# Low parts last, a late unit behind the squares, transposes one piece later: reordering the passes of a split-float32 encoder trunk

## The chip, the cores and the metric

The kernel runs on one core of a Trainium2 chip, in one launch. The metric is the device time of the execution in microseconds (us). The matrix engine is called TensorE (PE in the profile; its loads of the stationary operand are PEld), the others are VectorE (DVE), ScalarE (ACT), GpSimd (POOL) and SyncE (SP), whose queue starts the transfers.

## The reference, cut to what matters

Two layers work on 256 tokens of 1024 numbers. Each layer has parallel branches, a feed-forward part and an embedding part, with a norm before and behind each.

```python
def hybrid_layer(h, p_i, ...):
    u = rms_norm(h, g_mix_pre)
    (gq, gk, gv, gg, ra_f, ra_b, aq, ak, av, gate_a, gate_b) = jnp.split(u @ w_in, offsets, axis=-1)
    # branch A: gated linear attention, both directions, times silu(gg), @ w_o_gla
    # branch B: grouped-query attention with rotary positions, @ w_o_attn
    mixed = jax.nn.sigmoid(gate_a) * branch_a + jax.nn.sigmoid(gate_b) * branch_b
    h = h + rms_norm(mixed @ w_out, g_mix_post)

    gate, up = jnp.split(rms_norm(h, g_ffn_pre) @ w_ffn_in, 2, axis=-1)
    h = h + rms_norm((jax.nn.silu(gate) * up) @ w_ffn_out, g_ffn_post)

    e = p_i @ w_ple_proj
    h = h + rms_norm(jax.nn.sigmoid(h @ w_ple_gate) * e, g_ple_post)
    return h
```

Everything is float32.

## The kernel before, in words

**Products in three passes.** Every float32 operand of a large product is split into a high part (a rounded copy, `fp32r`) and a low part (the rest). A product x*y is the sum of three passes on TensorE: xh*yh, xh*yl and xl*yh. `mm3` issues these three for one block of 128 of the inner dimension, and the next block follows. `split` makes the parts: ScalarE copies to the high part (`nc.scalar.copy`, line 118, a CAST in the profile), and VectorE subtracts it from the source to make the low part (`vsub`, line 114). A low part is thus always made after its high part.

**Units of weights.** The weights come as units: 2048 (in the rank/query stage 2112) columns of 128 rows, four blocks of 128 by 512, 1 MB. A plan lists the units in the order of use. `Stream` moves them: a transfer fills a `raw` buffer (two of them), `put` takes a pair of places `wh` and `wl` (four pairs), and `fill` splits the unit in two pieces of half its columns. `take` hands out the next unit, and `done` says that its last product has been issued: it counts the unit out (`held`), starts transfers that have room, and calls `fill`, which splits the next unit as long as fewer than `depth` (4, at times 3) are held. A raw buffer is free for the next transfer when VectorE has made the low part of its second piece.

**Products.** The tokens are two halves (`hf` 0 and 1) of 128. `amode` multiplies one half's activations with 512 or 256 columns of one unit; the activations are the stationary operand. `wmode` takes the weights as the stationary operand. `times` is used for the seven products of a block scheme, `rq_step` for the first stage of a layer (ranks and queries), where a step is one unit of one half, in three blocks of 288, 384 and 384 columns, two blocks of the inner dimension each, 18 passes in all. `by_half` is used for the output projection (`wout`) and for the embedding gate (`gate`, tiles named `ple` in the profile): it takes four units, does the first token half with all of them, then the second half, and there the second 512 columns are done as two pieces of 256. Each unit is counted out in the second half, as its last piece ends. `then` follows each half: `after_out` or `after_gate`, a norm behind the product, the addition to `h` and the norm before the next product.

**Norm chain.** The norm (`row_rstd`, `pre_norm`, `post_norm_add`) takes the squares of two halves of a row on ScalarE (line 460), an addition and a power on GpSimd (lines 472 and 476), and a scaling on VectorE (line 480 ahead of the next product, 520 for the addition to `h`). The result is transposed on TensorE (`transpose_in`, line 422) and split into the activations of the next product. `last_square` keeps the last square that was issued.

**Order.** The order of each engine's queue is set when the kernel is built: instructions of earlier program order go first when they are ready by a modelled time, `tc.high_priority` moves the norm chains ahead, and `tc.issue_after(x)` holds an instruction behind x in its engine's queue. Deferred work (transposes above all) lives in tasks; a product calls `tick` after each half unit, or after each 256-column piece or each block of `rq_step`, and a task that was told to wait n ticks issues its work at the n-th. The constants `WAIT...` at the top are these numbers. In the layer change, `pre_norm(gnext, hf, nxt, (WAIT, WAIT_NEXT)[hf])` gives the first half's transposes 6 ticks and the second half's 9. Of the second half's gate pieces each 512-column one gives two ticks and each 256-column one gives one, eight in all. The steps of layer 1's first stage are, as half and unit, `00 01 02 10 03 11 12 13`.

## Time and profile before

| | |
|---|---|
| median of 3 runs | 929.62 us (928.83 to 929.95) |
| the profiled execution | 930.95 us |
| its span, first to last instruction | 929.2 us |
| mean granted TensorE clock | 0.996 |
| TensorE busy | 915.3 us, 4669 passes and transposes |
| loads of the stationary operand | 777.1 us, 4669 |
| VectorE busy | 787.3 us |
| ScalarE busy | 580.5 us |
| GpSimd busy | 88.1 us |
| read from memory | 167.41 MB, 181 GB/s over the span |

Busy times come from the one profiled execution. Matmuls overlap in it and their ends are modelled, so starts are the better measure: the time from one start to the next. A row of the timeline gives the start, the length, the engine, the line and operation, output and inputs by the program's names (`wl_0ple` is a low part that was made in layer 0 in the part `ple`), the shapes, the count of instructions merged into the row, and in brackets the idle time before it with what ended it.

### The profile page before, as it was taken

The page shows a single profiled execution, that of the slowest core. Times are in us where ns is not written, and L with a number is a line of the kernel's source. Part 1 is how long each engine was busy: PE and PEld are TensorE (multiplying, and loading weights), DVE is VectorE, ACT ScalarE, POOL GpSimd, SP SyncE. Part 2 cuts the span into 40 slices and gives each one's busy share as a digit, 9 for nine tenths or more (in the row PEclk, how much of TensorE's full clock was granted, in tenths as well). Part 3 has the DMA queues.
Part 4 walks back from the last instruction along what each step waited for, and adds up shares of the span by engine and source line. Part 5 has one row for each costly group of instructions (what it writes and reads, how often), then busy time and mean ns, then how long its engine had stood idle before and what let it go on. Part 6 is the DMA issues. An engine that isn't in the chain of part 4 may idle for free.

```text
span 929.2 us, 12392 instructions
## 1 busy us (share of the span) xinstructions
PE 915.3 (99%) x4669; PEld 777.1 (84%) x4669; DVE 787.3 (85%) x1002; ACT 580.5 (62%) x955; POOL 88.1 (9%) x147
## 2 busy tenths in 40 slices
PE   8999999999999999999999999999999999999996
PEld 6898888888878888888889988888888788888886
DVE  6898989987679898998779789899786899989974
ACT  4669676664466565666656686755545666655663
POOL 3400212310000000001022002200001000000000
PEclk9999999999999999999999999999999999999999
DMA  7463445556385564627545525354663847473551
GB/s 264 138 240 122 154 164 187 178 201 230 107 271 190 182 245 174 228 102 268 182 138 182 185 88 172 113 214 139 246 226 114 287 139 265 159 256 129 182 182 45
DMA packets 88247, 169.25 MB, mean 182 GB/s; under 512 B 3374, under 2 KB 26550, under 8 KB 88188
## 3 DMA queue, kind: packets, MB, share of 16 engines
q1 hardware_dynamic: 88028, 168.32, 52.4%
q8 instruction: 36, 0.59, 0.3%
q10 hardware_dynamic: 160, 0.15, 0.1%
q14 instruction: 23, 0.19, 0.1%
HBM read 167.41 MB, written 1.05 MB: 181 GB/s over the span
## 4 chain that ended last, share of the span: by engine, by line
PE 89%; DVE 3%; DMA 2%; ACT 2%; POOL 2%; issue 2%; SPq 0%; POOLq 0%; DVEq 0%; ACTq 0%
PE acc_0ffnin L102 11%; PE acc_1ffnin L102 11%; PE acc_0ffnin L566 6%; PE acc_1ffnin L566 6%; PE acc_0gate L102 5%; PE acc_1gate L102 5%; PE acc_1gqk L102 2%; PE acc_0gqk L102 2%; PE acc_1ple L102 2%; PE acc_0gg L102 2%; PE acc_1gg L102 2%; PE acc_1v L102 2%; PE acc_0v L102 2%; PE acc_1merge L102 2%; PE acc_0merge L102 2%; PE acc_1gate L566 2%
## 5 line engine op out<-in xcount | busy, mean ns | idle before, releaser
L102 PE MATMUL acc_1ffnin<-wh_1ffnin,big_1ffnin 128*128 128x512 f32 x176 | 56.8, 392 | 0.0
L102 PE MATMUL acc_0ffnin<-wh_0ffnin,big_0ffnin 128*128 128x512 f32 x176 | 56.8, 392 | 0.0
L118 ACT CAST wh_0ffnin<-raw_0ffnin 128x1024 fp32r<-128x1024 f32 x38 | 38.2, 1050 | 23.9 <-DVE wl_0ffnin L114 6.9
L114 DVE TENSOR_TENSOR wl_0ffnin<-raw_0ffnin,wh_0ffnin 128x1024 fp32r<-128x1024 f32 x38 | 44.9, 1220 | 8.3 <-ACT wh_0ffnin L118 8.3
L118 ACT CAST wh_1ffnin<-raw_1ffnin 128x1024 fp32r<-128x1024 f32 x38 | 38.1, 1049 | 21.6 <-DMA raw_1ffnin<-in_w_ffn_out_dram 7.0
L114 DVE TENSOR_TENSOR wl_1ffnin<-raw_1ffnin,wh_1ffnin 128x1024 fp32r<-128x1024 f32 x38 | 44.9, 1221 | 7.3 <-ACT wh_1ffnin L118 7.2
L102 PEld LDWEIGHTS acc_1ffnin<-wh_1ffnin,big_1ffnin 128*128 128x128 f32 x176 | 33.0, 188 | 6.7
L102 PEld LDWEIGHTS acc_0ffnin<-wh_0ffnin,big_0ffnin 128*128 128x128 f32 x176 | 33.0, 188 | 6.7
L114 DVE TENSOR_TENSOR wl_1ffnin<-lent_1ffnin,wh_1ffnin 128x1024 fp32r<-128x1024 f32 x30 | 35.9, 1219 | 1.9 <-ACT wh_1ffnin L118 1.9
L114 DVE TENSOR_TENSOR wl_0ffnin<-lent_0ffnin,wh_0ffnin 128x1024 fp32r<-128x1024 f32 x30 | 35.9, 1219 | 1.7 <-ACT wh_0ffnin L118 1.7
L102 PE MATMUL acc_0ffnin<-wl_0ffnin,big_0ffnin 128*128 128x512 f32 x88 | 34.3, 389 | 0.0
L102 PE MATMUL acc_1ffnin<-wl_1ffnin,big_1ffnin 128*128 128x512 f32 x88 | 34.3, 389 | 0.0
L118 ACT CAST wh_1ffnin<-lent_1ffnin 128x1024 fp32r<-128x1024 f32 x30 | 30.2, 1053 | 6.5 <-PE acc_1ffnin L102 3.0
L118 ACT CAST wh_0ffnin<-lent_0ffnin 128x1024 fp32r<-128x1024 f32 x30 | 30.1, 1053 | 6.0 <-PE acc_0ffnin L102 3.0
L566 PE MATMUL acc_0ffnin<-wh_0ffnin,mid_0ffnin 128*128 128x512 f32 x96 | 31.1, 391 | 0.0
L566 PE MATMUL acc_1ffnin<-wh_1ffnin,mid_1ffnin 128*128 128x512 f32 x96 | 31.1, 391 | 0.0
L102 PE MATMUL acc_1ffnin<-wh_1ffnin,big_1wout 128*128 128x512 f32 x96 | 31.0, 393 | 0.0
L102 PE MATMUL acc_0ffnin<-wh_0ffnin,big_0wout 128*128 128x512 f32 x96 | 31.0, 393 | 0.0
L114 DVE TENSOR_TENSOR wl_1gate<-raw_1gate,wh_1gate 128x1024 fp32r<-128x1024 f32 x20 | 23.6, 1220 | 6.2 <-ACT wh_1gate L118 6.1
L114 DVE TENSOR_TENSOR wl_0gate<-raw_0gate,wh_0gate 128x1024 fp32r<-128x1024 f32 x20 | 23.8, 1234 | 5.2 <-ACT wh_0gate L118 5.2
L118 ACT CAST wh_1gate<-raw_1gate 128x1024 fp32r<-128x1024 f32 x20 | 20.2, 1051 | 12.7 <-DMA raw_1gate<-in_w_o_attn_dram 6.4
L118 ACT CAST wh_0gate<-raw_0gate 128x1024 fp32r<-128x1024 f32 x20 | 20.1, 1052 | 12.2 <-DMA raw_0gate<-in_w_o_attn_dram 5.9
(697 smaller groups left out, 2999.1 us busy)
## 6 DMA issues: line engine op xcount, KB each, us to landing
raw_0ffnin<-in_w_ffn_out_dram SPq DMA_DIRECT2D x11, 1024.0 KB, 5.1
raw_1ffnin<-in_w_ffn_out_dram SPq DMA_DIRECT2D x11, 1024.0 KB, 5.8
lent_0ffnin<-in_w_ffn_in_dram SPq DMA_DIRECT2D x6, 1024.0 KB, 7.5
lent_1ffnin<-in_w_ffn_in_dram SPq DMA_DIRECT2D x6, 1024.0 KB, 7.5
raw_0v<-in_w_in_dram SPq DMA_DIRECT2D x4, 1024.0 KB, 4.9
raw_0gate<-in_w_o_gla_dram SPq DMA_DIRECT2D x4, 1024.0 KB, 5.0
raw_0gate<-in_w_o_attn_dram SPq DMA_DIRECT2D x4, 1024.0 KB, 5.5
raw_0wout<-in_w_ffn_in_dram SPq DMA_DIRECT2D x8, 512.0 KB, 4.6
```

Source lines behind the costliest of these rows:

```text
L102: return nc.tensor.matmul(o, lhsT, rhs, start=start, stop=stop)
L114: nc.vector.tensor_tensor(out=out, in0=in0, in1=in1, op=ALU.subtract)
L118: nc.scalar.copy(hi, src)
L566: nc.tensor.matmul(o, x, y, start=first and k + n == 0, stop=k == 3 and n == 2, skip_group_check=not first)
```

## The change

Three things are changed.

1. `passes` takes the place of `mm3` in `amode`, `wmode`, `times` and `rq_step`. It issues the same passes in another order: for each block of the inner dimension the two passes that do not use the part named last, and behind all blocks the passes with that part. With `fresh` that part is the low part of the first operand (the activations, or in `wmode` the weights), otherwise the low part of the second (the weights, where the activations are stationary). `fresh` is set for the first 512 columns in `by_half`, for the first block of the feed-forward part, for the first unit in `rq_step`, and in `wmode`. `rq_first`, `out_step` and the attention keep their order. The ticks stay where they were: after half of the passes and at the end.
2. `by_half` is called with `early`. The last unit that it counts out is no longer refilled at once: `fill` runs after `then` of the second half, and the ScalarE copies of the unit it splits are held behind the last square. A class `Early`, counts of large tiles and a flag `go` are added, by which units could be split into large tiles ahead of time; no item of the plan is such a unit.
3. In the layer change the first half's transposes wait 7 ticks instead of 6.

```diff
-WAIT, WAIT_FIRST, WAIT_NEXT, WAIT_H, WAIT_FFN, WAIT_BLOCK = 6, 4, 9, 5, 4, 6
+WAIT, WAIT_FIRST, WAIT_H, WAIT_FFN, WAIT_BLOCK = 6, 4, 5, 4, 6
+
+WAIT_NEXT = 7, 9
...
+    def passes(o, parts, start, stop, fresh=False, between=None, **kw):
+        ps = [((xh, yh), (xh, yl), (xl, yh)) if fresh else ((xh, yh), (xl, yh), (xh, yl)) for (xh, xl), (yh, yl) in parts]
+        seq = [p for t in ps for p in t[:2]] + [t[2] for t in ps]
+        for n, (x, y) in enumerate(seq):
+            nc.tensor.matmul(o, x, y, start=start and n == 0, stop=stop and n == len(seq) - 1, **kw)
+            if between is not None and 2 * (n + 1) == len(seq):
+                between()
...
-        def fill(self):
-            while self.open and self.held < self.depth and self.jobs:
+        def fill(self, behind=None):
+            while self.open and self.jobs and (self.go if self.jobs[0] in self.early else self.held < self.depth):
                 pieces = self.jobs.pop(0)()
-                for piece in pieces or ():
-                    split(*piece)
+                for hi, lo, src in pieces or ():
+                    with tc.issue_after(behind) if behind is not None else nullcontext():
+                        nc.scalar.copy(hi, src)
+                    vsub(lo, src, hi.bitcast(F32))
                 if pieces:
                     self.load()
...
-        def done(self, n=1):
-            self.held -= n
+        def done(self, n=1, late=False):
+            self.go = False
+            for _ in range(n):
+                self.held -= self.taken.pop(0)
             self.start()
-            self.fill()
+            if not late:
+                self.fill()
...
-    def amode(o, sp, hf, k0, w, first, last, c0=0):
+    def amode(o, sp, hf, k0, w, first, last, c0=0, fresh=False):
...
-        for k in range(4):
-            mm3(o, sp.tok(k0 + k, hf), (wh[:, k, :], wl[:, k, :]), first and k == 0, last and k == 3)
-            if k % 2 and (k == 3 or o.shape[-1] == 512):
-                tick()
+        parts = [(sp.tok(k0 + k, hf), (wh[:, k, :], wl[:, k, :])) for k in range(4)]
+        passes(o, parts, first, last, fresh, tick if o.shape[-1] == 512 else None)
+        tick()
...
-    def by_half(sp, then):
+    def by_half(sp, then, early=False):
...
-                    amode(t, sp, hf, kh * 4, us[kh, min(j, 1)], kh == 0, kh == 1, 256 * (j == 2))
+                    amode(t, sp, hf, kh * 4, us[kh, min(j, 1)], kh == 0, kh == 1, 256 * (j == 2), j == 0)
+                    if hf == 0 and kh == 1 and early:
+                        ws.go = True
+                        ws.fill()
                     if hf == 1 and j != 1:
-                        ws.done()
+                        ws.done(late=early and (kh, j) == (1, 2))
             then(hf, o)
+        if early:
+
+            ws.fill(last_square[0].ins)
...
-            for k in range(2):
-                s = slice(k * 1056 + c0, k * 1056 + c1)
-                mm3(
-                    o[:, : c1 - c0], uT.tok(2 * u + k, hf), [t[:, s] for t in us[u]],
-                    u == 0 and k == 0, u == 3 and k == 1,
-                )
+            s = [slice(k * 1056 + c0, k * 1056 + c1) for k in range(2)]
+            parts = [(uT.tok(2 * u + k, hf), [t[:, s[k]] for t in us[u]]) for k in range(2)]
+            passes(o[:, : c1 - c0], parts, u == 0, u == 3, u == 0)
             tick()
...
-        by_half(mixT, after_out)
+        by_half(mixT, after_out, True)
...
-                pre_norm(gnext, hf, nxt, (WAIT, WAIT_NEXT)[hf])
+                pre_norm(gnext, hf, nxt, WAIT_NEXT[hf])
...
-        by_half(hT, after_gate)
+        by_half(hT, after_gate, True)
```

More of the change, by code (lines that the diff above doesn't have):

```diff
@@ L283, in put @@
         def put(self, x, parts=2):
[L285 to L288 removed]
             cuts = [slice(j * x.n // parts, (j + 1) * x.n // parts) for j in range(parts)]
+            if x.bigs == 4:
+                ts = [big(F32R)[:, : x.n // parts] for _ in range(4)]
+                self.ready.append((ts[0:2], ts[2:4], 0))
+                return [(ts[j], ts[2 + j], x.raw[:, c]) for j, c in enumerate(cuts)]
+            if x.bigs:
+                wh, wl = big(F32R), big(F32R)
+            else:
+                wh = wp.tile([P, UNIT], F32R, tag="wh", name=nm("wh"))
+                wl = wp.tile([P, UNIT], F32R, tag="wl", name=nm("wl"))
+                self.held += 1
+            self.ready.append((wh, wl, not x.bigs))
             return [(wh[:, c], wl[:, c], x.raw[:, c]) for c in cuts]
@@ L548, in wmode @@
             s = slice(f * P, (f + 1) * P)
-            for k in range(4):
-                mm3(
-                    o, (wh[:, k, s], wl[:, k, s]), sp.all(k0 + k),
-                    first and k == 0 and f % 2 == 0, last and k == 3 and f % 2 == 1,
-                )
+            parts = [((wh[:, k, s], wl[:, k, s]), sp.all(k0 + k)) for k in range(4)]
+            passes(o, parts, first and f % 2 == 0, last and f % 2 == 1, True)
             tick()
@@ L561, in times @@
         wh, wl = (t[:, :2048].rearrange("p (k c) -> p k c", c=512) for t in ws.take())
-        for k in range(4):
-            (ah, al), h, lo = act(k), wh[:, k, :], wl[:, k, :]
-            for n, (x, y) in enumerate(((ah, h), (ah, lo), (al, h))):
-                nc.tensor.matmul(
-                    o, x, y, start=first and k + n == 0, stop=k == 3 and n == 2, skip_group_check=not first
-                )
-            if k % 2:
-                tick()
+        parts = [(act(k), (wh[:, k, :], wl[:, k, :])) for k in range(4)]
+        passes(o, parts, first, True, between=tick, skip_group_check=not first)
+        tick()
         if then:
```

28 lines of the change are left out of this document (15 added, 13 removed).

## The prediction

> **What bounds the kernel now.** First the page's part on busy time, then the waits of TensorE, then two stretches by windows, then the timelines of the places that the waits name.
>
> ```profile
> PE 915.3 (99%) x4669; PEld 777.1 (84%) x4669; DVE 787.3 (85%) x1002; ACT 580.5 (62%) x955; POOL 88.1 (9%) x147
> ...
> 297.04 2.72 PE acc_0ffnin L102 x12
> ...
> 68.17 5.76 PE acc_0gqk L102 x48
> ...
> 488.76 5.80 PE acc_1rq L102 x36
> ```
>
> TensorE is the bound: what is not its work is at most some ten microseconds. The three lines below it, from the chain of waits, give the pitch of its passes: 2.72 / 12 = 0.227 us for 512 columns, 5.76 / 48 = 0.12 us for 256, and 5.80 / 36 = 0.161 us in the rank/query stage (288 and 384 columns mixed). The change neither adds nor removes a pass, so it can win only where TensorE stands still.
>
> ```profile
> PE acc_1rq L102 <- DVE wl_0ple L114: 1.4, 2, 0.9
> ...
> PE aux_0ple L422 <- DVE mid_0ple L480: 0.8, 2, 0.5
> ...
> PE acc_0kv L102 <- DVE wl_0rq L114: 0.5, 1, 0.5
> PE acc_0ffnin L102 <- DVE wl_0wout L114: 0.2, 1, 0.2
> PE acc_1ffnin L102 <- DVE wl_1wout L114: 0.2, 1, 0.2
> ...
> 256.00:270.00 14.00, 13.62 (x62) 10.40 (x61) 11.26 (x16) 11.32 (x22) 2.02 (x5) 1.00 0.73 221
> ...
> 474.50:482.00 7.50, 5.59 (x26) 4.71 (x25) 5.06 (x9) 4.76 (x12) 1.44 (x3) 0.77 0.47 157
> ```
>
> These are all of TensorE's waits but three in the first stage (us in total, times, longest); none lies in the feed-forward blocks. Four of these five are waits for `wl`, the low part of a weight unit, which VectorE makes after ScalarE's copy `wh`. The last two lines are stretches (length, then busy time of PE, PEld, DVE, ACT, POOL, then the granted clock). At 474.5 to 482, where layer 1 begins, TensorE is idle 7.50 - 5.59 = 1.91 us and its clock is 0.77, another 0.23 x 7.50 = 1.73 us lost: **3.6 us** in one place. At 256 to 270 the clock stayed at 1.00 with 0.38 us idle. The Trainium skill (TensorE: Matmul & The Clock Gate, Part 1) says the array falls to half rate after an idle window of about 3.4 us. The trace agrees in size: 0.77 over 7.5 us is half rate for 3.45 us.
>
> **Layer 1's beginning: transposes one piece later (A).**
>
> ```profile
> 461.04 1.42 DVE L480 SCALAR_TENSOR_TENSOR mid_0ple<-h,rstd_0ple,mid_0ple 128x512 f32<-128x512 f32 x2 [0.85 <-POOL rstd_0ple L476]
> ...
> 461.17 0.39 PE L102 MATMUL acc_0ple<-wh_0ffnout,big_0ffnout 128*128 128x512 f32 x1
> 461.85 1.38 PE L422 MATMUL aux_0ple<-ident,mid_0ple 128*128 128x128 f32 x8 [0.29 <-DVE mid_0ple L480]
> ...
> 251.80 1.03 PE L422 MATMUL aux_0wout<-ident,mid_0wout 128*128 128x128 f32 x8
> ```
>
> The first token half's eight transposes stand after six ticks of the second half's gate pieces. TensorE is free at 461.17 + 0.23 = 461.40 and starts them at 461.85 (0.45 us), and they take 1.38 us instead of the 1.03 us of the same eight elsewhere (0.35 us): 0.80 us lost to the norm's scaling (461.04 to 462.46). With 7 ticks a 256-column piece of 12 x 0.12 = 1.44 us comes first, the transposes start at 462.84, and the scaling is done. Behind them stands one more such piece, 1.44 us, in which the casts to the high part must finish before the first rank/query pass: one cast is some 0.6 us, and the low part is wanted only after four passes, since these passes count as fresh. So **-0.75 us**, from -0.8 to +0.2, the upper end if another ScalarE instruction of about a microsecond gets ahead of the cast.
>
> **The last unit behind the squares (B).**
>
> ```profile
> 472.97 1.08 ACT L118 CAST wh_0ple<-raw_0ple 128x1056 fp32r<-128x1056 f32 x1 [3.06 <-DMA raw_0ple<-in_w_in_dram]
> 473.96 0.63 ACT L460 ACTIVATE t_0ple<-h 128x512 f32<-128x512 f32 x1
> ...
> 474.58 1.06 ACT L118 CAST wh_0ple<-raw_0ple 128x1056 fp32r<-128x1056 f32 x1
> 475.54 0.63 ACT L460 ACTIVATE t_0ple<-h 128x512 f32<-128x512 f32 x1
> ...
> 476.28 1.28 ACT L837 ACT_TABLE_LOAD   x1
> ...
> 471.72 1.41 DVE L520 SCALAR_TENSOR_TENSOR h<-mid_0ple,rstd_0ple,h 128x512 f32<-128x512 f32 x2 [0.85 <-POOL rstd_0ple L476]
> 474.09 1.26 DVE L114 TENSOR_TENSOR wl_0ple<-raw_0ple,wh_0ple 128x1056 fp32r<-128x1056 f32 x1 [0.95 <-ACT wh_0ple L118]
> ...
> 477.79 1.42 DVE L480 SCALAR_TENSOR_TENSOR mid_0ple<-h,rstd_0ple,mid_0ple 128x512 f32<-128x512 f32 x2 [0.86 <-POOL rstd_0ple L476]
> ...
> 474.46 0.47 PE L102 MATMUL acc_1rq<-wh_0ple,big_0ple 128*128 128x384 f32 x2
> 475.40 0.40 PE L102 MATMUL acc_1rq<-wl_0ple,big_0ple 128*128 128x288 f32 x1 [0.47 <-DVE wl_0ple L114]
> ...
> 476.99 0.40 PE L102 MATMUL acc_1rq<-wl_0ple,big_0ple 128*128 128x288 f32 x1 [0.90 <-DVE wl_0ple L114]
> ...
> 478.59 1.11 PE L422 MATMUL aux_0ple<-ident,mid_0ple 128*128 128x128 f32 x4 [0.55 <-DVE mid_0ple L480]
> ```
>
> The second half's `h` is ready at about 472.47 and 473.13 (two of 0.7 us from 471.72), but ScalarE stands in front of its squares with the copy of the fourth rank/query unit, waiting 3.06 us for its transfer, and puts the other copy between the squares. So the squares end at 476.17 and the scaling starts at 477.79, 1.62 us later (GpSimd's add and power).
>
> After the change the copies are held behind the second square. The squares run from about 472.5 to 473.85, and the scaling can start at 473.85 + 1.62 = 475.5. The copies end at about 475.0 and 476.0 (two of 1.0 us) instead of 474.0 and 475.6. VectorE takes either the scaling first or, as in the trace, the first low part (475.0 to 476.25); so the first transposes can start between 476.25 and 477.05 instead of 478.59.
>
> TensorE ends the three steps before at about 474.8 - 0.75 = 474.05 and waits for the first copy, 0.95 us. In the old order a block's second pass wants `wl`; these are the waits at 475.40 and 476.99. In the new one 12 of the step's 18 passes want only `wh`: 12 x 0.161 = 1.93 us of work, until 476.95, when the transposes are there. I add 0.5 us for the cast behind them. So 1.45 us stays of 3.6 us: -2.15 us, of which I take **-2.0**. The best end is -2.6 (only the wait for the copy). The worst is that the transposes stand at the head of TensorE's queue: it then waits from 474.05 to 477.05, and at the clock loss of before that is 3.0 + 1.73 = 4.7 us, +1.1. I stand near the good end, because before, too, passes of this step were queued ahead of the transposes. Behind the copies on ScalarE wait the table load (1.28 us, 476.0 to 477.3) and the casts of these transposes, which come no earlier anyway; VectorE's low parts end up to 2.4 us later, and the transfer into their place as much, for a unit of the next stage but one step; its first pass lies over 10 us on (the steps left are four of 18 passes, 2.9 us each).
>
> At the two output projections the same edit is worth **0**:
>
> ```profile
> 261.63 0.63 ACT L460 ACTIVATE t_0wout<-h 128x512 f32<-128x512 f32 x1
> ...
> 263.02 2.00 ACT L118 CAST wh_0wout<-raw_0wout 128x1024 fp32r<-128x1024 f32 x2 [0.67 <-DMA raw_0wout<-in_w_ffn_in_dram]
> ...
> 266.03 0.50 PE L102 MATMUL acc_0ffnin<-wl_0wout,big_0wout 128*128 128x512 f32 x1 [0.18 <-DVE wl_0wout L114]
> 266.37 0.62 PE L102 MATMUL acc_0ffnin<-wh_0wout,big_0wout 128*128 128x512 f32 x2
> ```
>
> The last unit's copies stand behind the last square already, because its transfer lands later. In layer 1's gate no unit is left. `Early` is used by no item of the plan, so the fill it would allow in the first half never runs.
>
> **Low parts last (C, F, E).** The rows just shown give C: a pass that wants `wl` starts at 266.03 with 0.18 us seen idle, and the next comes 0.34 us later instead of 0.227. The pass ahead started at 265.38, so the whole loss is 266.03 - 265.61 + 0.11 = 0.53 us. In the new order the first `wl` pass is the ninth, 1.6 us later; gone. Layer 1 has the same wait, so **-1.0 us** for both, between -1.06 and 0.
>
> F is the second key/value unit of layer 0:
>
> ```profile
> 35.56 1.06 ACT L118 CAST wh_0rq<-raw_start 128x1024 fp32r<-128x1024 f32 x1
> ...
> 37.26 1.08 ACT L118 CAST wh_0rq<-raw_start 128x1024 fp32r<-128x1024 f32 x1
> ...
> 42.38 1.22 DVE L114 TENSOR_TENSOR wl_0rq<-raw_start,wh_0rq 128x1024 fp32r<-128x1024 f32 x1
> ...
> 43.66 0.50 PE L102 MATMUL acc_0kv<-wl_0rq,big_start 128*128 128x512 f32 x1 [0.54 <-DVE wl_0rq L114]
> ...
> 23.90 0.69 DVE L128 TENSOR_TENSOR big_start<-t_start,big_start 128x512 fp32r<-128x512 f32 x1 [0.68 <-ACT big_start L128]
> ...
> 23.92 0.40 PE L102 MATMUL acc_0rq<-wh_start,big_start 128*128 128x288 f32 x1 [0.54 <-ACT big_start L128]
> ```
>
> Both copies are ready by 38.34, the first low part only at 43.60; 16 of the 24 passes can now run before it, 3.6 us. **-0.6 us** (0.54 idle and 0.1 for the restart; -0.8 to 0). E is the price: in the first rank/query stage the activations of the last four blocks are the late part, and these passes do not count as fresh, so the activations' low part (23.90 to 24.59) is wanted at the second pass of a block instead of the third. Three blocks give three passes first, 0.48 us from 23.92: **+0.2 us**, 0 to 0.6.
>
> Against the order itself the Trainium skill (TensorE: Matmul & The Clock Gate, Step-by-step) says that one load of the stationary operand can serve several matmuls. The old order put two passes with one stationary operand side by side, and the new one often parts them; by that rule loads would be added. The page's first line has a load for each pass already, 4669 to 4669, so by the row it costs nothing.
>
> **Sum.** -0.75 - 2.0 - 1.0 - 0.6 + 0.2 = -4.15 us. The profiled execution took 930.95 us (span 929.2 us), 1.33 us over the median of 929.62 us, so 926.8 us in its terms and 929.62 - 4.15 = **925.5 us** as a median.
>
> **Rivals.**
> 1. *The transposes stand at the head and the clock falls again.* B is +1.1 instead of -2.0: -0.75 + 1.1 - 1.0 - 0.6 + 0.2 = -1.05, 928.6 us. For it: the window at 474.5 with its 0.77. Against: the passes that now fill the wait. By the Trainium skill (TensorE: Matmul & The Clock Gate, Part 1) half rate would come only if the idle time fills its window of about 3.4 us; 3.0 us is just short. 0.14.
> 2. *The late split brings nothing* (the copies and the table load behind the squares cost as much as the earlier squares win): B is 0, -2.15 us, 927.5 us. For it: the transfer lands at 472.95, after the first half of `h`. 0.12.
> 3. *The high halves become the late part.* In the new order the second half of `wh` is wanted at the fifth pass instead of the seventh, 2 x 0.227 = 0.45 us earlier. Where the second copy of a feed-forward unit ends less than that ahead of its pass, TensorE waits up to 0.45 us a unit. It decides from about 14 such units on: 925.5 + 14 x 0.45 = 931.8 us, slower. Against: TensorE has no wait in these blocks now. 0.10.
>
> **How the numbers follow.** The forecast has 0.64. A measurement of this kernel can tell 0.2% (1.86 us) from no change: under 927.76 us lie the forecast and rival 2, 0.76 faster; rival 1 is within, 0.14; rival 3 slower, 0.10. The low end is the best of each term (-0.8 - 2.6 - 1.06 - 0.8 = -5.3) and the spread of the runs, some 0.6: 923.7 us. The high end is rival 1 with that spread: 929.3 us.
>
> **What would show it.** Right: the squares of `t_0ple<-h` of the second half end near 473.9 by the old clock and ahead of both copies; the window there has a clock of 1.00 and under 1.5 us idle; `wl_0wout`, `wl_1wout` and `wl_0rq` are gone from TensorE's waits. Wrong: new TensorE waits for `wh` or for activations' low parts in the feed-forward blocks, or the clock below 1 after 474.

## The result, and the profile after

| | before | after |
|---|---|---|
| median of 18 runs each, on one chip | 929.89 us (928.83 to 931.07) | 927.90 us (926.90 to 930.30) |
| after / before | | 0.9981, 95% interval 0.9974 to 0.9988 |
| the profiled execution | 930.95 us | 927.04 us |
| its span | 929.2 us | 925.3 us |

The change brought 2.0 us where 4.15 had been forecast; 925.5 had been predicted and 927.9 came. On three other occasions the ratio was 0.9971 (0.9959 to 0.9983), 0.9981 (0.9972 to 0.9990) and 0.9969 (0.9958 to 0.9981). Yet the two profiled executions lie 3.91 us apart, close to the forecast. That these two differences disagree is the first thing to explain.

The page of the kernel after, busy time of TensorE:

```profile
PE 911.8 (99%) x4669; PEld 775.3 (84%) x4669; DVE 785.6 (85%) x1002; ACT 578.7 (63%) x955; POOL 83.2 (9%) x147
```

TensorE's waits after (us in total, times, longest), from the second on:

```profile
PE aux_0ple L459 <- DVE mid_0ple L517: 1.4, 1, 1.4
...
PE aux_0wout L459 <- DVE mid_0wout L517: 0.4, 1, 0.4
...
PE acc_1rq L120 <- DVE big_0ple L128: 0.2, 1, 0.2
PE aux_1at L104 <- DVE mid_1at L128: 0.2, 1, 0.2
```

All waits for a weight unit's low part are gone: `wl_0ple`, `wl_0rq`, `wl_0wout`, `wl_1wout`. What stands there now are waits for norm chains and for low parts of activations. The windows of after (length, busy PE, PEld, DVE, ACT, POOL, granted clock):

```profile
256.00:270.00 14.00, 13.50 (x65) 10.77 (x64) 11.27 (x16) 10.03 (x18) 1.71 (x4) 1.00 0.70 229
466.00:482.00 16.00, 14.49 (x88) 13.39 (x88) 10.85 (x17) 9.67 (x24) 3.02 (x8) 1.00 0.53 185
474.50:482.00 7.50, 7.35 (x46) 6.57 (x45) 5.12 (x9) 4.01 (x12) 0.22 (x1) 1.00 0.42 140
```

From 474.5 on TensorE is nearly always busy and its clock is whole, where before it was 0.77. But the wait has only moved ahead: 1.51 us are idle in the 16 us from 466. The timeline of after shows it:

```profile
462.49 1.25 DVE L128 TENSOR_TENSOR wl_0ple<-raw_0emb,wh_0ple 128x1056 fp32r<-128x1056 f32 x1
463.66 1.28 DVE L128 TENSOR_TENSOR big_0ple<-aux_0ple,big_0ple 128x512 fp32r<-128x512 f32 x2
463.80 0.37 SPq L298 DMA_DIRECT2D raw_0ple<-in_w_in_dram  x1
464.39 0.71 PE L120 MATMUL acc_1rq<-wh_0ple,big_0ple 128*128 128x288 f32 x3 [0.22 <-DVE big_0ple L128]
...
470.06 1.41 DVE L557 SCALAR_TENSOR_TENSOR h<-mid_0ple,rstd_0ple,h 128x512 f32<-128x512 f32 x2 [0.84 <-POOL rstd_0ple L513]
...
470.84 0.63 ACT L497 ACTIVATE t_0ple<-h 128x512 f32<-128x512 f32 x1 [2.59 <-DVE h L557]
471.60 0.63 ACT L497 ACTIVATE t_0ple<-h 128x512 f32<-128x512 f32 x1
472.23 2.03 ACT L362 CAST wh_0ple<-raw_0ple 128x1056 fp32r<-128x1056 f32 x2
473.40 1.42 DVE L517 SCALAR_TENSOR_TENSOR mid_0ple<-h,rstd_0ple,mid_0ple 128x512 f32<-128x512 f32 x2 [1.93 <-POOL rstd_0ple L513]
474.21 1.32 PE L459 MATMUL aux_0ple<-ident,mid_0ple 128*128 128x128 f32 x8 [1.37 <-DVE mid_0ple L517]
474.74 2.42 DVE L128 TENSOR_TENSOR wl_0ple<-raw_0ple,wh_0ple 128x1056 fp32r<-128x1056 f32 x2
```

The squares come as soon as `h` is there and ahead of both copies, as the prediction said. But the transposes now stand at the head of TensorE's queue right behind step 02, and it waits for them, 1.37 us by this row. And one thing has turned round that the prediction did not see: ScalarE no longer waits 3 us for the fourth unit's transfer, it waits 2.59 us for `h`. With the first half's transposes one piece later, VectorE makes the second unit's last low part (462.49) ahead of the activations' low part, not behind it, and so frees the `raw` buffer sooner: the transfer starts 6.26 us ahead of the second half's addition to `h` (463.80 and 470.06). In the kernel before it is 5.06 us (466.57 and 471.63 in experiment 1). So the late split holds back a unit that, as experiment 4 shows, is there before `h`.

### The profile page after: what moved, and what is told of

It is laid out like the page before. It is cut to its first block, busy times and chain, and to the rows that moved or that the text cites. A ratio compares the mean times of both kernels' runs of the same rounds, so it can differ in the third digit from the quotient of the medians.

```text
span 925.3 us, 12405 instructions
## 1 busy us (share of the span) xinstructions
PE 911.8 (99%) x4669; PEld 775.3 (84%) x4669; DVE 785.6 (85%) x1002; ACT 578.7 (63%) x955; POOL 83.2 (9%) x147
## 4 chain that ended last, share of the span: by engine, by line
PE 88%; DVE 4%; ACT 2%; DMA 2%; issue 2%; POOL 1%; SPq 0%; POOLq 0%; DVEq 0%; ACTq 0%
PE acc_1ffnin L120 11%; PE acc_0ffnin L120 11%; PE acc_1gate L120 7%; PE acc_0gate L120 7%; PE acc_0ffnin L104 6%; PE acc_1ffnin L104 6%; PE acc_0gqk L120 2%; PE acc_1gqk L120 2%; PE acc_1ple L120 2%; PE acc_1gg L120 2%; PE acc_0gg L120 2%; PE acc_0v L120 2%; PE acc_1merge L120 2%; PE acc_0merge L120 2%; PE acc_1rq L120 1%
## 5 line engine op out<-in xcount | busy, mean ns | idle before, releaser
L362 ACT CAST wh_1ffnin<-raw_1ffnin 128x1024 fp32r<-128x1024 f32 x32 | 32.3, 1049 | 24.6 <-DMA raw_1ffnin<-in_w_ffn_out_dram 7.7
L362 ACT CAST wh_0ffnin<-raw_0ffnin 128x1024 fp32r<-128x1024 f32 x32 | 32.4, 1049 | 24.1 <-DMA raw_0ffnin<-in_w_ffn_out_dram 7.0
L120 PE MATMUL acc_1ffnin<-wh_1ffnin,big_1wout 128*128 128x512 f32 x168 | 42.5, 393 | 0.0
L120 PE MATMUL acc_0ffnin<-wh_0ffnin,big_0wout 128*128 128x512 f32 x168 | 42.5, 393 | 0.0
L120 PEld LDWEIGHTS acc_0ffnin<-wh_0ffnin,big_0wout 128*128 128x128 f32 x168 | 31.1, 188 | 6.2
L120 PEld LDWEIGHTS acc_1ffnin<-wh_1ffnin,big_1wout 128*128 128x128 f32 x168 | 31.1, 188 | 6.2
L362 ACT CAST wh_1gate<-raw_1gate 128x1024 fp32r<-128x1024 f32 x18 | 18.0, 1049 | 11.3 <-DMA raw_1gate<-in_w_o_attn_dram 5.4
L362 ACT CAST wh_0gate<-raw_0gate 128x1024 fp32r<-128x1024 f32 x18 | 18.0, 1048 | 11.3 <-DMA raw_0gate<-in_w_o_attn_dram 5.4
```

What stands on the lines that cost most here:

```text
L120: nc.tensor.matmul(o, x, y, start=start and n == 0, stop=stop and n == len(seq) - 1, **kw)
L362: nc.scalar.copy(hi, src)
```

## The experiments

Each median below stands beside the median of the kernel before from the same chip, measured in turn with it.

**How losses are counted.** For each of the 4669 passes I took its start less the start of the one before and less the pitch for its width (0.227 us for 512 columns, 0.175 for 384, 0.133 for 288, 0.120 for 256, 0.109 for 128). The sums, us per stretch, worked out from the traces:

| stretch (term) | before, 930.95 and 931.17 | before, 929.90 and 929.60 | after, six profiles | passes alone, two |
|---|---|---|---|---|
| 0 to 100 (F, E) | 7.30 | 7.23 | 6.79 | 6.69 |
| 100 to 240 | 1.09 | 1.09 | 0.77 | 0.77 |
| 240 to 300 (C) | 1.43 | 1.46 | 1.25 | 1.10 |
| 400 to 466 (A) | 0.90 | 0.86 | 0.55 | 0.87 |
| 466 to 490 (B) | 4.21 | 2.94 | 2.52 | 1.90 |
| 530 to 600 | 0.72 | 0.87 | 1.12 | 1.11 |
| 700 to 800 (C) | 1.34 | 1.38 | 0.93 | 0.94 |
| the rest | 1.03 | 0.82 | 0.74 | 0.78 |
| sum | 18.02 | 16.65 | 14.68 | 14.15 |
| mean time | 931.06 | 929.75 | 927.70 | 927.18 |

The sums differ as the times do (the last line is the mean of the profiled executions): 1.37 and 1.31 us between the first two columns, 1.97 and 2.05 to after, 0.53 and 0.52 to the passes alone.

**1. The kernel before, three more profiles.**

> The kernel before, unchanged, for a second profile of it. Theory (the sum was made against an execution that lies above its own median, because the clock fell to half rate at the layer change: window 474.5 to 482 at 0.77): another execution near 929.5 us shows a granted clock of 0.95 or more in that window and some 1.7 us less lost there than the 3.6 us of the first profile; the waits of layer 0 and at 461.9 are the same as before (0.7 us there, 1.35 us at the output projection, 0.8 us at the step-00 rank units). Rival (the half rate at the layer change is in every execution, and the kernel after gives its gain back elsewhere): the clock in that window is again below 0.85 even where the time is near 929.5 us.

> The kernel before again, for one more profile. Both profiles of it so far (930.95 and 931.17 us) lie 1 us above its medians, and both have the layer change (474.5 to 482) at a granted clock of 0.77 with 4.2 us lost between 466 and 490. Theory (its executions are of two kinds, and the fall of the clock at the layer change makes the difference): an execution of 929 to 930 us shows a clock of 0.95 or more there and about 1.7 us less lost; one near 931 shows 0.77 again. Rival (the clock falls there in every execution and the spread comes from elsewhere, such as the first transfers): 0.77 at any time.

> The kernel before, a fourth profile. Theory: above 930.7 us with a clock of 0.77 in 474.5 to 482 and 4.2 us lost between 466 and 490, or below 930.3 with a clock of 1.00 and 2.9 us lost. Rival (time and clock there are not tied): one of the crossed pairs.

They took 931.17, 929.90 and 929.60 us. A window of the first of them, and below it two of the last:

```profile
474.50:482.00 7.50, 5.57 (x26) 4.68 (x25) 5.05 (x9) 4.94 (x12) 1.30 (x2) 0.77 0.48 161
```

```profile
466.00:482.00 16.00, 14.01 (x87) 13.02 (x86) 12.56 (x21) 8.96 (x20) 4.13 (x9) 1.00 0.59 200
474.50:482.00 7.50, 5.51 (x34) 4.52 (x33) 5.94 (x11) 4.64 (x12) 2.20 (x4) 1.00 0.45 149
```

The timeline of the last one:

```profile
466.57 10.75 SPq L275 DMA_DIRECT2D raw_0ple<-in_w_in_dram  x3
...
471.63 1.42 DVE L520 SCALAR_TENSOR_TENSOR h<-mid_0ple,rstd_0ple,h 128x512 f32<-128x512 f32 x2 [0.84 <-POOL rstd_0ple L476]
...
472.97 1.08 ACT L118 CAST wh_0ple<-raw_0ple 128x1056 fp32r<-128x1056 f32 x1 [3.15 <-DMA raw_0ple<-in_w_in_dram]
...
475.40 0.40 PE L102 MATMUL acc_1rq<-wl_0ple,big_0ple 128*128 128x288 f32 x1 [0.55 <-DVE wl_0ple L114]
...
476.98 0.40 PE L102 MATMUL acc_1rq<-wl_0ple,big_0ple 128*128 128x288 f32 x1 [0.89 <-DVE wl_0ple L114]
...
478.58 0.65 PE L422 MATMUL aux_0ple<-ident,mid_0ple 128*128 128x128 f32 x4 [0.55 <-DVE mid_0ple L480]
```

The same waits, within a tenth of a microsecond, as in the profile that the prediction was made from, but with the whole clock behind them. So the clock falls at the layer change in some executions and not in others (the last section has what decides it): two of the four profiles have 0.77 there and took 931 us, two have 1.00 and took 929.6 to 929.9. Time and clock went together each time, as the theory had it. The price is 4.21 - 2.94 = 1.27 us, less than the 1.73 us that the prediction read from the window, in part because TensorE still waits as the half rate begins (0.45 us busy in the first microsecond below). In the first profile, by microseconds, the half rate lasts one stretch of some 3.4 us:

```profile
478.00:479.00 1.00, 0.45 (x3) 0.41 (x3) 1.00 (x2) 0.00 (x0) 0.00 (x0) 0.65 0.94 205
479.00:480.00 1.00, 1.00 (x6) 0.93 (x5) 0.58 (x4) 0.26 (x1) 0.00 (x0) 0.50 0.97 360
480.00:481.00 1.00, 1.00 (x7) 1.00 (x5) 0.64 (x1) 0.68 (x4) 0.00 (x0) 0.50 1.03 401
481.00:482.00 1.00, 1.00 (x6) 1.00 (x6) 0.52 (x2) 0.77 (x3) 0.14 (x1) 0.64 0.20 76
```

**2. The order of the passes alone.** The kernel after with

```
-WAIT_NEXT = 7, 9
+WAIT_NEXT = 6, 9
-        by_half(mixT, after_out, True)
+        by_half(mixT, after_out)
-        by_half(hT, after_gate, True)
+        by_half(hT, after_gate)
```

> The kernel after with the order of the passes alone: no late split, and the first half's transposes one piece earlier again as in the kernel before. Terms C, F and E of the prediction are left: -1.0 -0.6 +0.2 = -1.4 us. Theory: 1.2 to 1.6 us under the kernel before (about 928.4), the waits for wl_0wout, wl_1wout and wl_0rq at the output projections and at step 00 gone, and the layer change as in the kernel before. Rival (these terms were over-counted, since a wait removed comes back a few instructions later): 0 to 0.7 us under the kernel before.

> The order of the passes alone, a second time, beside the kernel after on one chip. Theory: 0.5 to 1.0 us under the kernel after and 2.7 to 3.2 us under the kernel before. Rival (the first result, of six runs, was chance): the same as the kernel after.

Measured: 927.24 us beside 930.36 before (0.9960, 0.9948 to 0.9973), and later 927.12 beside 930.21 (0.9964, 0.9952 to 0.9976). The terms C, F and E forecast 1.4 us; this is 3.1, and 2.57 against the profiles of before that have the whole clock. It is also better than the whole change: beside it the kernel after had 927.88 and 928.32 us, 0.64 and 1.20 us more. TensorE's waits of the second run, its window, and two rows of the first run's timeline:

```profile
PE aux_0ple L459 <- DVE mid_0ple L517: 1.0, 2, 0.7
...
PE acc_1rq L120 <- DVE wl_0ple L128: 0.4, 1, 0.4
```

```profile
466.00:482.00 16.00, 14.94 (x93) 14.19 (x92) 11.89 (x21) 9.89 (x24) 4.14 (x9) 1.00 0.60 200
```

```profile
465.52 9.81 SPq L298 DMA_DIRECT2D raw_0ple<-in_w_in_dram  x3
...
470.98 1.08 ACT L362 CAST wh_0ple<-raw_0ple 128x1056 fp32r<-128x1056 f32 x1 [2.20 <-DMA raw_0ple<-in_w_in_dram]
```

Without any late split, one of the two waits for `wl_0ple` is gone and the other is down to 0.6 and 0.4 us, the clock is whole in both profiles, and 1.90 us are lost in the mean, less than the 2.52 us of the kernel after. Two things differ from before: passes that want only `wh` stand in front, and the fourth unit's transfer takes 5.5 us from its issue to the copy that waits for it (465.52 to 470.98), against 6.4 us in the last profile of before (466.57 to 472.97); why it is quicker was not found. Experiment 5 tests the first alone.

**3. The late split and the later transposes alone.** The kernel after with the old order of the passes:

```
-        seq = [p for t in ps for p in t[:2]] + [t[2] for t in ps]
+        seq = [p for (xh, xl), (yh, yl) in parts for p in ((xh, yh), (xh, yl), (xl, yh))]
```

> The kernel after with the old order of the passes: the late split and the later transposes alone, terms A and B. The prediction has -2.75 us for them (927.1). Theory (of B's 3.6 us, 1.73 us were a fall of the clock that the typical execution does not have, and a new 1.5 us wait for the transposes takes most of the rest): 0.3 to 1.0 us under the kernel before (about 929.2). Rival (A and B bring what the trace-to-trace comparison says, 2.06 us, and the passes bring nothing in the median): 1.8 to 2.8 us under it.

Measured: 929.66 us beside 930.36 (0.9993, 0.9982 to 1.0003). Its profile, 929.37 us, loses 0.08 us from 400 to 466 and 3.04 us from 466 to 490, at a whole clock. An execution of before with a whole clock has 0.86 and 2.94. So A and B together win 0.68 us there, where the prediction had 2.75. The waits of this profile at the layer change:

```profile
466.19 0.53 PE L119 MATMUL acc_1rq<-wh_0ple,big_0ple 128*128 128x288 f32 x2 [0.49 <-DVE big_0ple L127]
...
476.01 1.32 PE L458 MATMUL aux_0ple<-ident,mid_0ple 128*128 128x128 f32 x8 [1.13 <-DVE mid_0ple L516]
...
477.84 0.40 PE L119 MATMUL acc_1rq<-wl_0ple,big_0ple 128*128 128x288 f32 x1 [0.38 <-DVE wl_0ple L127]
```

The waits at 461.85 and 462.60 are gone, and one at 466.19 for the activations' low part has come (0.65 us lost); of the three waits behind 474 two others are left, the longer one for the transposes at the head of the queue.

**4. Two of the three parts.** Without the late split (the two `by_half` lines of experiment 2), and without the later transposes (its `WAIT_NEXT` line):

> The kernel after without the late split: the order of the passes and the first half's transposes one piece later. Theory (the passes' order by itself took the waits and the fall of the clock at the layer change away, so that the late split only adds the wait of 1.5 us for the transposes behind step 02): as the passes alone less 0.3 to 0.7 us of the waits at 461, which is 3.2 to 3.8 us under the kernel before and 0.7 to 1.2 us under the kernel after. Rival 1 (the later transposes do the harm, the late split none): as the kernel after, 2.0 to 2.5 us under the kernel before. Rival 2 (without the late split the second half's norm chain ends 2 us later): 1.5 us or less under the kernel before.

> The kernel after with the first half's transposes one piece earlier again, as in the kernel before: the order of the passes and the late split. Theory (the late split adds about 0.5 us at the layer change over the passes alone, and the waits of 0.7 us for the first half's transposes are back): 2.0 to 2.6 us under the kernel before, like the kernel after or up to 0.5 us behind it. Rival (the late split brings its 2 us also on top of the passes, and the later transposes undo it): 3.5 us or more under the kernel before.

Measured beside 930.38: without the late split 929.21 us (0.9989, 0.9980 to 0.9998), without the later transposes 928.15 us (0.9973, 0.9964 to 0.9983). For the second the theory held: it is like the kernel after. For the first it failed: it should have been the best of all, and it is some 2 us behind the passes alone (1.2 us under the kernel before, where these had 3.1). Its timeline and window:

```profile
469.08 2.05 ACT L362 CAST wh_0ple<-raw_0ple 128x1056 fp32r<-128x1056 f32 x2 [0.57 <-DMA raw_0ple<-in_w_in_dram]
...
470.31 1.41 DVE L557 SCALAR_TENSOR_TENSOR h<-mid_0ple,rstd_0ple,h 128x512 f32<-128x512 f32 x2 [0.84 <-POOL rstd_0ple L513]
...
471.64 2.42 DVE L128 TENSOR_TENSOR wl_0ple<-raw_0ple,wh_0ple 128x1056 fp32r<-128x1056 f32 x2
...
474.83 1.41 DVE L517 SCALAR_TENSOR_TENSOR mid_0ple<-h,rstd_0ple,mid_0ple 128x512 f32<-128x512 f32 x2 [0.77 <-POOL rstd_0ple L513]
...
475.64 0.66 PE L459 MATMUL aux_0ple<-ident,mid_0ple 128*128 128x128 f32 x4 [2.15 <-DVE mid_0ple L517]
```

```profile
474.50:482.00 7.50, 6.36 (x32) 6.28 (x33) 3.08 (x6) 1.63 (x3) 0.30 (x1) 0.77 0.43 140
```

The fourth unit's copies begin 1.23 us ahead of the addition to `h` (469.08 and 470.31), both its parts are made by 474.06, and yet TensorE stands still for 2.15 us: three passes of step 03 were queued ahead of the transposes, one between them and the other fourteen behind. Here the clock fell again. So the three parts are not additive: each of A and B moves the place of the transposes in TensorE's queue, because that place is set from modelled ready times when the kernel is built. The passes alone leave seven of step 03's high passes and two low ones ahead of them, A alone on top leaves three, B alone on top none, A and B together none.

**5. The passes in one loop alone.** In the kernel with the passes alone, the old order everywhere but in layer 1's `rq_step`:

```
+        if not last:
+            seq = [p for (xh, xl), (yh, yl) in parts for p in ((xh, yh), (xh, yl), (xl, yh))]
...
+            passes(..., u == 0, last=l == 1)
```

> The kernel before in everything but one place: in layer 1's rank and query units alone the products of the parts made last come last (no late split, transposes as before, the other loops in the old order). Theory (it is this, and not the late split, that takes the waits for wl_0ple and the fall of the clock at the layer change away): 1.5 to 2.3 us under the kernel before, 1.9 to 2.0 us lost between 466 and 490 at a clock of 1.00, the waits at 43.7, 264 and 266 as before. Rival (the passes' gain at the layer change comes from the earlier stages, which shift the times there): 0.5 us or less under the kernel before.

Measured: 929.79 us beside 930.21 (0.9995, 0.9986 to 1.0004): the rival's 0.5 us or less. Its profile, 929.79 us, loses 2.72 us from 466 to 490 at a whole clock, 0.22 us less than before at a whole clock:

```profile
466.81 10.48 SPq L300 DMA_DIRECT2D raw_0ple<-in_w_in_dram  x3
...
472.94 1.08 ACT L364 CAST wh_0ple<-raw_0ple 128x1056 fp32r<-128x1056 f32 x1 [2.86 <-DMA raw_0ple<-in_w_in_dram]
```

Here the transfer takes 6.1 us, and the high passes themselves now wait for the copy. So the order in this loop does not do it alone: it wins 0.22 of the 1.04 us that the passes everywhere win at this place (2.94 to 1.90). There the unit comes sooner as well, and that the rest is due to this was not shown.

**6. The wait filled.** The kernel after with six idle passes of ones ahead of the second half's transposes, written into the accumulator that these overwrite:

```
+        if part[0] == "0ple" and hf == 1 and k == 0:
+            for i in range(6):
+                nc.tensor.matmul(ps, keep[:, 0:P], keep, start=True, stop=True)
```

> The kernel after with six idle passes of 512 columns (ones, into the accumulator that the transposes then overwrite) between step 02 and the second half's transposes, so that TensorE works through most of the 1.5 us wait at 474.2. Theory (the upper executions of the kernel after, some 2 us above the others, are those in which the clock falls behind that wait): the lower executions stay within 0.3 us of the kernel after's lower ones (927 to 928.3), and those above 929 are gone or down to one in twelve. Rival (their time lies elsewhere): a quarter to a third of the executions above 929, as in the kernel after.

> The kernel after, a third time. 2.0 to 2.5 us under the kernel before; a quarter of its executions some 2 us above the others. If the profile is one of those: by theory a clock of 0.77 to 0.9 somewhere behind the 1.5 us wait for the transposes; by the rival a transfer that is waited for.

> The kernel after, unchanged. Theory: median 927.5 to 928.3 us as before, with a lower cluster near 927.3 and some executions near 929.6; the profile, if it falls into the lower cluster, shows the same 1.5 us wait at 474.2 with a clock of 1.00 behind it; if it falls into the upper one, some 2 us more are lost in one place, by the theory behind that wait at a clock below 0.85. Rival (the upper executions lose their time to transfers that land late): the extra time lies in a wait for a DMA, at a clock of 0.99.

> The kernel after, beside the kernel with the filled wait. 927.9 to 928.4 us, a quarter to a third of its executions above 929. If its profile is one of those, the theory has a granted clock of 0.77 to 0.9 behind the wait at 474; the rival a longer wait somewhere at a full clock.

> The kernel after, one more profile. If its time is above 929: by theory a granted clock below 0.9 behind the wait at 474.5 (about 1.3 us) and the wait as before; by the rival a longer wait elsewhere at a full clock. If it is 927 to 928.4: as the four profiles before, 2.4 us lost between 466 and 490 at a clock of 1.00.

> As the run before it: one more profile of the kernel after, with the same two readings if its time is above 929.

Filled: 928.95 us beside 930.19 (0.9988, 0.9979 to 0.9996), 4 of 11 executions above 929. The kernel after, beside it: 927.53 us, none of 7. The experiment does not decide, by a flaw of its own: the passes behind the transposes came in another order, with waits of 0.58 and 0.78 us at 476.4 and 478.0 in the place of the one filled. The other runs of the kernel after had 927.88 us (1 of 6 above 929), 928.32 (4 of 12), and in two single executions 927.67 and 927.93. All its six profiles, 927.04 to 928.33 us, have the whole clock at the layer change and lose 2.50 to 2.53 us from 466 to 490. What its executions of 929 to 931 us lose, and where, was not caught and stays open. One part of the spread can be seen: in 6 of the 20 profiles (two of after, one of before, three of other versions) the clock also falls to half for 3.4 us between 8 and 13 us from the start, and those lose 2.7 us from 8 to 20 us in the mean, the others 1.9.

**7. Another late split.** First, with the kernel after: the first piece split as soon as it has landed, the second behind the last square, and step 03 ahead of step 10:

```
-STEPS = "00 01 02 10 03 11 12 13".split()
+STEPS = "00 01 02 03 10 11 12 13".split()
-WAIT_NEXT = 7, 9
+WAIT_NEXT = 7, 10
...
+            if hf == 1 and early and ws.open and ws.held < ws.depth and ws.jobs:
+                first, rest = ws.jobs.pop(0)()
+                split(*first)
             then(hf, o)
+            if rest:
+                hi, lo, src = rest
+                with tc.issue_after(last_square[0].ins):
+                    nc.scalar.copy(hi, src)
+                vsub(lo, src, hi.bitcast(F32))
+                ws.load()
```

> The kernel after with the last rank/query unit split in two steps (its first piece as soon as it has landed, where ScalarE is idle for 2.6 us ahead of the squares; its second piece behind the last square) and step 03 ahead of step 10 in TensorE's queue, so that the transposes of the second half come some five passes of step 03 later. Theory (the 1.5 us wait at 474.2 is an empty queue: the norm chain ends at 474.2 and nothing else may run before it): 0.7 to 1.3 us less lost there, 3 to 3.6 us under the kernel before and about 1 us under the kernel after. Rival (the squares move behind the first piece and the chain ends later by the same amount): the same time as the kernel after, within 0.3 us.

Measured: 929.21 us beside 930.38 (0.9986, 0.9977 to 0.9995), 1.2 us under the kernel before, where the kernel after had 1.9 to 2.7. Neither theory nor rival. VectorE puts the second low part behind the norm's scaling, and a pass that wants it stands ahead of five of the eight transposes and of all that follows:

```profile
475.59 1.25 DVE L128 TENSOR_TENSOR wl_0ple<-raw_0ple,wh_0ple 128x1056 fp32r<-128x1056 f32 x1
...
476.90 0.40 PE L120 MATMUL acc_1rq<-wl_0ple,big_0ple 128*128 128x288 f32 x1 [1.29 <-DVE wl_0ple L128]
```

So, from the kernel with the passes alone (transposes early as before, steps as before), at the layer change only, with that low part held ahead of the scaling:

```
+    def second_piece():
+        if rest[0]:
+            (hi, lo, src), rest[0] = rest[0], None
+            with tc.issue_after(last_square[0].ins):
+                nc.scalar.copy(hi, src)
+            low = nc.vector.tensor_tensor(out=lo, in0=src, in1=hi.bitcast(F32), op=ALU.subtract)
+            ws.load()
+            return low
...
             r = row_rstd(x)
+            low = second_piece()
             for j, y in enumerate(halves(xn)):
-                scale_gain(y, x[j], r, gs[j])
+                with tc.issue_after(low.ins) if low is not None else nullcontext():
+                    scale_gain(y, x[j], r, gs[j])
```

> The order of the passes, and at the layer change alone a late split of another kind: the last rank/query unit's first piece is split as soon as it has landed, its second piece is copied behind the last square on ScalarE, and on VectorE its low part comes ahead of the norm's scaling. Step 03's two first blocks stand ahead of the transposes in TensorE's queue. Theory (what is lost at the layer change is a queue whose head waits while other passes are ready: 0.79 us for the low part and 0.84 us for the transposes in the run with the passes alone): 1.0 to 1.6 us less lost between 466 and 490 than with the passes alone, so 0.4 to 0.9 us there in all and 3.8 to 4.6 us under the kernel before. Rival (the squares move behind the first piece's copy, and the chain ends as late): as the passes alone, within 0.3 us.

> The version of the late split with the second piece alone behind the squares and its low part ahead of the scaling, a second time. From the profile, which lost 0.9 us less between 466 and 490 than the mean of the two with the passes alone: 0.5 to 0.9 us under the passes alone, so 3.6 to 4.0 us under the kernel before. Rival (what the median showed: no more than the passes alone): 3.0 to 3.3 us.

Measured: 927.01 us beside 930.21 (0.9965, 0.9953 to 0.9977), where the passes alone had 927.12, and the second time 926.35 us beside 930.19 (0.9956, 0.9943 to 0.9968), where the kernel after had 927.53. The timeline and the window of the second run:

```profile
470.87 1.42 DVE L561 SCALAR_TENSOR_TENSOR h<-mid_0ple,rstd_0ple,h 128x512 f32<-128x512 f32 x2 [0.84 <-POOL rstd_0ple L513]
...
471.81 0.62 ACT L497 ACTIVATE t_0ple<-h 128x512 f32<-128x512 f32 x1
...
472.56 0.64 ACT L497 ACTIVATE t_0ple<-h 128x512 f32<-128x512 f32 x1
...
473.19 1.06 ACT L697 CAST wh_0ple<-raw_0ple 128x1056 fp32r<-128x1056 f32 x1
...
474.28 1.26 DVE L698 TENSOR_TENSOR wl_0ple<-raw_0ple,wh_0ple 128x1056 fp32r<-128x1056 f32 x1 [0.82 <-ACT wh_0ple L697]
...
474.80 0.86 PE L120 MATMUL acc_1rq<-wh_0ple,big_0ple 128*128 128x384 f32 x4
...
475.45 1.41 DVE L517 SCALAR_TENSOR_TENSOR mid_0ple<-h,rstd_0ple,mid_0ple 128x512 f32<-128x512 f32 x2
...
476.35 0.60 PE L459 MATMUL aux_0ple<-ident,mid_0ple 128*128 128x128 f32 x4
```

```profile
466.00:482.00 16.00, 15.94 (x99) 15.07 (x98) 13.36 (x24) 10.73 (x27) 4.75 (x11) 1.00 0.60 200
```

TensorE is busy 15.94 of 16.00 us there, against 14.49 in the kernel after and 14.94 with the passes alone; 1.00 us is lost from 466 to 490 in the mean of its two profiles (925.88 and 926.44 us). The norm chain is 1.2 us longer than in the kernel after (from the addition to `h` to the scaling 475.45 - 470.87 = 4.58 us, there 473.40 - 470.06 = 3.34) and costs nothing, because thirteen passes of step 03 stand ahead of the transposes. This is the best version found, 1.3 and 1.2 us under the kernel after, beside which it ran both times. That it beats the passes alone is seen in the profiles (0.9 us less lost at the layer change); the medians of the one occasion where both ran are 0.11 us apart, and the intervals overlap.

## Why the prediction was wrong

The step that failed is the sum, by what it took for B. It was made against the profiled execution of 930.95 us and then subtracted from the median of 929.62 us. That is sound only for losses that both have, and B's half rate was not in every execution. The other half of the step is the transposes: they were taken to stand behind 12 passes of step 03, and stood ahead of all 18.

- **The clock in B.** 1.73 of B's 3.6 us were the half rate at 474.5 to 482. In the four profiles of before it was there twice, with 931 us, and absent twice, with 929.75 us in the mean; it is worth 1.3 us, about what the prediction noted as the distance of its execution from the median (1.33 us) and did not ask about. In what share of the executions it falls is not known; the later medians of before, 930.19 to 930.38 us, lie between the two kinds. In that execution's own terms it forecast 926.8 us, and the profiled execution of after took 927.04. That this is so close is in part luck: it is the shortest of after's six, whose mean is 927.70.
- **The rest of B.** The forecast kept 1.45 us with its 0.5 for the cast, and 1.51 us are idle from 466 to 482 (in the table's terms 4.21 - 2.0 = 2.2 us would have been left, and 2.52 were lost). That the sizes are so near is luck: the forecast had them for the first copy and the cast, and they are the wait for the transposes. These went to the head of TensorE's queue: the first half of rival 1, which had 0.14, without the fall of the clock that it priced along with it (the whole clock in all six profiles) and with a chain that ended at 474.2 and not at 477.05. That "before, too, passes of this step were queued ahead" was no evidence: that order came from when the parts were modelled as ready, and B itself changed this. Against executions with the same clock B is -0.42 us instead of -2.0. On top of the new order of the passes even that is not its own: A and B together leave 0.6 us more at this place than the passes alone, and 0.3 us less at 461. Rival 2, that the late split brings nothing, came closest with 927.5 us, but not for its reason: the earlier squares did win (from the addition to `h` to the scaling 3.34 us, before 6.07), and TensorE's queue gave it away.
- **A**, -0.75: -0.31. The waits at 461.85 and 462.60 went as forecast, but VectorE put a weight unit's low part (462.49) ahead of the activations' low part (463.66), and a pass waited at 464.39. The prediction had watched ScalarE for this, not VectorE. A's other effect, the transfer that starts 1.2 us sooner by the time of `h`, was missed: it took away the stall that B was costed against.
- **C**, -1.0: -0.21 in layer 0 and -0.45 in layer 1, -0.66 us. The waits for `wl_0wout` and `wl_1wout` went; in layer 0 the wait of the transposes ahead of them grew instead (`aux_0wout`, 0.4 us in the first profile, whose window from 256 has 0.50 us idle against 0.38).
- **F and E**, -0.4: the stretch to 100 us has -0.44, and place by place both terms were about right: from 30 to 50 us the loss went from 0.83 to 0.04 us (F, `wl_0rq` is gone), from 20 to 30 us from 0.73 to 0.97 us (E). The rest of the stretch scatters by a microsecond from profile to profile.
- **Not foreseen**: -0.32 us from 100 to 240, in pieces of about 0.1, and +0.25 us from 530 to 600, where a pass at 544.84 now waits for `mid_1at`.

So, clock for clock, -0.31 - 0.42 - 0.66 - 0.44 - 0.32 + 0.25 = -1.90, and -0.08 in the rest: -1.98 us from the losses, -2.05 from the times of the profiles, -1.99 from the medians. The shape of the forecast held (nothing got slower, rival 3's waits for `wh` in the feed-forward blocks did not come); A, B and C were each too large, B by 1.6 us. Against the two profiles with the fall of the clock the change brought 18.02 - 14.68 = 3.34 us: of the 2.2 us that the medians lack of 4.15, 1.3 are the clock, and the rest is A, B and C being too large, less what was not foreseen.

## What to carry to other kernels

Before a loss in one profile is subtracted from a median, ask whether the median's executions have it: a profile 1.3 us above the median was the sign. One more may not settle it: here the second had the fall again, and the third and fourth did not. Parts of a change that touch the same wait are not additive; cost the second one against the kernel with the first one in it, and ask of every shift what it frees earlier, here a transfer's buffer. When a chain is made shorter, look at what stands ahead of its end in the waiting engine's queue: a chain 1.2 us longer, with ready passes ahead of its end, was better than the short one.

## What the runs showed of the hardware

The traces record when the granted clock changes. At the layer change each fall to half rate lasts 3.41 us, and in all 20 profiles the stretch from one change to the next inside the kernel is a whole multiple of 3.413 us (1, 130, 137, 138, 266 to 269 times). So the clock changes only at the borders of a grid of windows that runs on and does not start with a wait. Where the grid lies decides. In the two profiles of before with the fall, nearly all idle time of the three waits lies in one window (474.89 to 478.30 in the first), and TensorE is idle for 0.48 of it. In the other two a border parts the waits, and the windows are idle for 0.41 and 0.16, and for 0.37 and 0.21. The wait of 2.15 us in experiment 4 left a window idle for 0.63, and the clock fell; the kernel after's one wait of 1.4 us left none idle for more than 0.41, and it fell in none of six. So at the layer change it fell behind windows idle for 0.48 or more (3 profiles) and not behind 0.41 or less (17). In the first 13 us this does not sort the profiles: there it fell behind windows idle for 0.36 to 0.49, and not behind others idle for up to 0.48.

The Trainium skill (TensorE: Matmul & The Clock Gate, Part 1) speaks of a free-running window of about 3.4 us, and these traces agree. The same part of the Trainium skill asks for an idle window; here half a window was enough, and TensorE's longest wait in the lists of these runs is 2.2 us.
